# A four-layer decoder step: the scores of a pair of heads and the recurrent layer's sample part with full-array matrix products

## The chip, the cores and the metric

The kernel runs on one core of a Trainium2 chip, as one program. The metric is device time in microseconds (us), the median of several executions; lower is better. The engines are TensorE (PE in the profile, its weight loads PEld), VectorE (DVE), ScalarE (ACT), GpSimd (POOL) and SyncE (SP, which here issues nearly all DMAs). PE multiplies a stationary operand (at most 128 rows by 128 columns, loaded ahead of the product) with a moving one and adds into PSUM.

## What is computed

One inference step of a decoder with four layers of kinds A, B, C, A, for two groups that share the weights: a prompt of 256 tokens, and 8 samples of 8 new tokens each. The model is 2048 wide. Every layer is `x = x + mixer(rmsnorm(x)) @ w_out`, with an input projection that also makes a gate z.

```
A (attention):  32 heads of 64, 4 key heads; window 128; sink in the softmax
    prompt: blocks of 128 queries against the block itself and the one before
    s = q k / 8, masked;  p = softmax with sink;  o = p v
C (recurrent, 16 heads, keys 128, values 128, chunks of 32):
    b = cumsum(log f);  q_t = q exp(b);  k_intra = k exp(-b)
    o = q_t S + causal(q_t k_intra) v;   S' = exp(b_last) S + k_state v
    o = rmsnorm(o) * norm_g;   y = (silu(z) * o) @ w_out
```

Layer B is a gated convolution and is not touched. All is float32. The outputs are the last hidden states of both groups, the key and value windows, and the convolution and recurrent states.

## The kernel before

**Main stream.** Tokens lie along the free dimension: 256 of the prompt and 64 of the samples, 320 columns. `run_step` (L184 to L220) makes two output tiles of 128 features from 16 k tiles. Float32 weights and activations are split into an upper and a lower part that are exact in PE's float32r form (`w_split`, L167: ACT makes the upper part at L176, DVE or, in some steps, POOL the lower part at L177), and each product is three: upper by upper (L212), upper by lower (L213), lower by upper (L214). With 132 steps that is 12672 products of 128 x 128 weights with 320 columns. The weights stream from HBM in pieces of 128 x 1024; four raw, three upper and three lower pieces are held.

**Side work.** Everything else (rotary, scores, softmax, recurrence, gates, norms) is written as generators in eight lanes (`Lanes`), which are advanced a little at each tick of the main stream, so its small matrix products come to stand between the main ones. A pool of four PSUM slots `sm` serves them. The program is then put in order by a scheduler that simulates its time; each engine runs its own list in that order.

**Scores** (`att_unit`, L461). A unit takes one query tile `o` of a pair of key heads: 2 layers x 2 pairs x 4 groups x 2 tiles. The two heads of a pair lie on the upper and the lower 64 partitions. `qd[kv]` holds both parts of one head's queries on 128 partitions, `ql` the lower parts of both heads on their own halves; `kk` holds both parts of the keys, and `kb` only the upper parts, each head on its own half and zero elsewhere, so that one product with `ql` serves both heads. Before, `kb` is made for the first block of 128 keys (L372 to L374, L406). For the first block of queries L475 multiplies `ql` with `kb` (256 columns) and L477 adds one product a head. For the second block (256 keys a head) L480 multiplies `qd[kv]` with `kk`, and L481 adds, for each head, a product of 64 rows: the head's own half of `ql` with the same half of `kk`. L487 then adds the mask and takes the maximum on DVE.

**Recurrent layer** (`layer_c`, L792; `gla`, L930; `norm`, L1079). Each of 16 heads has three products on the samples' 64 tokens that are not full: L991 multiplies keys and queries (64 weight columns, 64 moving columns), L1017 the samples' attention with their values (64 weight columns), L1095 transposes 64 rows of the output. They are float32, which the profile shows as two records each, except for the transposes. L980 and L981 are the prompt's attention, L993 the state, L1014 to L1016 the prompt's output, L1093 and L1094 its transposes, L944 to L949 other transposes.

Of the kernel before, what the change touches and what calls it, by code (L numbers as in the profile page):

```python
# [18 lines left out]
NB = 8  # L19
# [9 lines left out]
LC_CM, LC_CMS, LC_SC, LC_BM, LC_BU, LC_ATS, LC_W, LC_AT, LC_END = 0, 128, 192, 512, 516, 524, 652, 652, 1164  # L29
# [3 lines left out]
class Pool:  # L33
    """A tag of a tile pool with a fixed number of slots, counted while tracing."""
# [29 lines left out]
class Lanes:  # L64
    """Side work traced between the matrix products of the main stream, a little at each tick."""
# [32 lines left out]
# steps in which Pool computes a share of the weights' lower parts: the vector engine has the attention to do  # L98
POOL_STEPS = set(range(2, 14)) | set(range(68, 86)) | set(range(108, 122))
# the softmax parts (head, query block) that the scalar engine normalizes  # L100
NORM_A = ((0, 0),)
# ticks between the stages of the side work
# [3 lines left out]
def trunk_kernel(ctx, tc, ins, outs):  # L106
# [77 lines left out]
    def run_step(getx, evac):  # L184
        """Two output tiles [128, NTOK]: 16 k tiles by 3 exact-part products each."""
# [7 lines left out]
        def order(k):  # L193
            # the program's last products: one tile ends before the other
            if final and k >= 12:
                return [(kk, k // 2 - 6) for kk in range(12 + 2 * (k % 2), 14 + 2 * (k % 2))] if k < 16 else []
            return [(k, 0), (k, 1)]
# [29 lines left out]
    def rsqrt(x, out, t, scratch_engine=None):  # L227
        """out = 1/sqrt(x), all [128, n] float32; x and t are overwritten."""
# [22 lines left out]
    def make_h(p, li, o):  # L251
        """Split x * ln_g of tile m into its exact parts, and add its squares up."""
# [35 lines left out]
    def split_y(p, o, y):  # L288
        """y float32 [128, NTOK] into the parts of tile (p, o)."""
        A.activation(out=yH[p][:, o, :], in_=y, func=ACTF.Copy)  # L290
        V.tensor_tensor(out=yL[p][:, o, :], in0=y, in1=yH[p][:, o, :].bitcast(F), op=ALU.subtract)
        ydone.add(2 * p + o)

    def evacuate(ps, words=NTOK):
        """The two output tiles times 1 / rms of their tokens."""
# [6 lines left out]
    def gate(w):  # L302
        """w = w (1 + tanh(w / 2)) = 2 silu(w)."""
# [52 lines left out]
    def layer_a(li):  # L356
# [7 lines left out]
        # cached keys, new keys, cached keys: the first of a pair of samples, and the second from the new keys on  # L364
# [3 lines left out]
        # keys (pair, head of the pair): exact parts over the partitions, the head's own half holds the upper one;  # L368
        # values (key block, pair, head of the pair): parts along the columns, in the same order
        kk = bg.get([128, 2, 2, TP], R)  # L370
        vp = bg.get([128, 2, 2, 2, 128], R)
        # the upper parts of the first key block, the two heads of a pair beside each other on their own halves  # L372
        kb = bg.get([128, 2, 2, 128], R)
        A.activation(out=kb, in_=ident.unsqueeze(1).to_broadcast([128, 4, 128]), func=ACTF.Copy, scale=0.0)  # L374
# [22 lines left out]
        def k_evac(ps):  # L397
            for o in range(2):
                yield from wait(wk, 2)
                a = rope(ps[o])  # L400
                for kv in range(2):
# [4 lines left out]
                    A.activation(out=kb[own, o, kv, :], in_=a[own, 0:128], func=ACTF.Copy)  # L406
# [6 lines left out]
            # the queries from here on are taken times -1/8: scores are negative, their minimum guards the softmax  # L413
# [47 lines left out]
        def att_unit(pr, gp, qd, ql):  # L461
# [5 lines left out]
            for o in range(2):  # L467
# [4 lines left out]
                # the first block of both heads and the second of the first, then the second of the second  # L472
                Sa, Sb = sm.get([128, 512]), sm.get([128, 256])
                S = [[Sa[:, 0:128], Sa[:, 256:512]], [Sa[:, 128:256], Sb]]
                T.matmul(out=Sa[:, 0:256], lhsT=ql[:, o, 0:128], rhs=kb[:, pr, :, :], start=True, stop=False)  # L475
                for kv in range(2):
                    T.matmul(out=S[kv][0], lhsT=qd[kv][:, o, 0:128], rhs=kk[:, pr, kv, 0:128], start=False, stop=(kv == 1))  # L477
                for kv in range(2):
                    sl = slice(64 * kv, 64 * kv + 64)
                    T.matmul(out=S[kv][1], lhsT=qd[kv][:, o, 128:256], rhs=kk[:, pr, kv, :], start=True, stop=False)  # L480
                    T.matmul(out=S[kv][1], lhsT=ql[sl, o, 128:256], rhs=kk[sl, pr, kv, :], start=False, stop=True)  # L481
                for kv in range(2):
# [7 lines left out]
                    sm.free()  # L490
# [63 lines left out]
        def smp_job(pr):  # L554
            while not (kdone[0] and vdone[0]):
                yield 1
            for hb in range(2):
                yield from wait(dyn, 9)
                # a pair of samples: cached keys, new keys of both, cached keys
# [6 lines left out]
                # the new values of four samples by token: upper, lower, upper parts  # L566
# [13 lines left out]
                for b2 in range(2):  # L580
# [41 lines left out]
                    # the pair's new keys are rows 16 * b2 and on: the mask clears the rest  # L622
# [169 lines left out]
    def layer_c(li):  # L792
# [4 lines left out]
        # the samples' attention, over the identity  # L797
        attss = [lc[:, LC_ATS + 64 * i:LC_ATS + 64 * i + 64] for i in range(2)]
        # the samples' queries for each half of the samples: columns (part, half, token), zero in the other half
# [36 lines left out]
        def c_pair(p):  # L836
# [18 lines left out]
            def f_evac(ps):  # L855
                yield from wait(wk, 5)
                ws = evacuate(ps)
                for o in range(2):
                    h = 2 * p + o
                    yield from wait(wk, 3)  # L860
                    q, f = st["q", o], ws[o]
# [15 lines left out]
                    st["k", o] = (ki, P)  # L877
# [9 lines left out]
        def gla_prep(h, q, ki, P, v):  # L887
# [3 lines left out]
            # products of the chunks' last decays: between chunks, to the end of a tile, from its start  # L891
# [447 lines left out]
```

## Time and profile before

| | |
|---|---|
| three runs | 2116.04, 2118.27, 2119.67 us; median 2118.27 |
| profiled execution | span 2113.5 us from the first to the last instruction; the page has no other time of it |
| busy | PE 2083.0 us (99%), weight loads 2040.2 (97%), DVE 1419.5 (67%), ACT 1007.6 (48%), POOL 684.8 (32%) |
| granted TensorE clock, mean | 0.995 of full speed |
| HBM | 153 GB/s over the span |

The page is of one execution. PE's products are pipelined, and a record's duration is not what the product costs: the next one starts well before its end. What a product costs is the time from its start to the start of the next, which the timeline shows; merged rows (x2, x4) stand for several records of one line. A product's form is given as rows * columns of its weights, then rows x columns of the moving operand (128*64 128x64: 128 rows and 64 columns of weights, 64 columns moving).

### The profile page before, as it was taken

To read this page: it belongs to the slowest core of one execution; us is meant where nothing else is said; L and a number is where in the kernel's file an instruction comes from. 1 tells how busy PE (TensorE), PEld (TensorE's weight loads), DVE (VectorE), ACT (ScalarE), POOL (GpSimd) and SP (SyncE) were. 2 spreads that over 40 slices of the span, in tenths; PEclk is the share of its full clock that TensorE was granted. 3 is DMA by queue.
4 is the path that set the end of the run, shared out by engine and by line. 5 is a ranking of instruction groups with operands and counts; after the bars stand their busy time and mean duration, and the time that the engine had idled before them with its cause. 6 is when DMAs were issued, how large, how long until landed. Compare 5 with 4: busy or idle time off the path is not lost.

```text
span 2113.5 us, 36996 instructions
## 1 busy us (share of the span) xinstructions
PE 2083.0 (99%) x14026; PEld 2040.2 (97%) x14026; DVE 1419.5 (67%) x2752; ACT 1007.6 (48%) x2034; POOL 684.8 (32%) x1002
## 2 busy tenths in 40 slices
PE   7999999999999999999999999999999999999997
PEld 7999999999999999999999999999999999999997
DVE  8778765564455545455878888888865677877644
ACT  5667654433333333344354544455444357675442
POOL 4676500110000000012545565435401156752010
PEclk9999999999999999999999999999999999999999
DMA  6433565444444444455454444454465543435542
GB/s 216 131 129 120 182 187 173 149 147 150 150 150 151 149 151 150 153 169 171 145 164 151 162 152 146 148 171 142 143 211 175 167 147 127 131 122 174 174 150 101
DMA packets 105866, 326.45 MB, mean 154 GB/s; under 512 B 16536, under 2 KB 24472, under 8 KB 105688
## 3 DMA queue, kind: packets, MB, share of 16 engines
q1 hardware_dynamic: 104968, 322.78, 48.0%
q8 instruction: 110, 1.80, 0.3%
q10 hardware_dynamic: 720, 1.31, 0.2%
q14 instruction: 68, 0.56, 0.1%
HBM read 301.88 MB, written 22.17 MB: 153 GB/s over the span
## 4 chain that ended last, share of the span: by engine, by line
PE 91%; DVE 6%; POOL 1%; issue 1%; ACT 0%; DMA 0%; SPq 0%; DVEq 0%; POOLq 0%; ACTq 0%
PE mm L214 27%; PE mm L213 27%; PE mm L212 27%; PE sm L518 1%; DVE wlp L177 1%; PE sm L481 1%; PE sm L540 1%; PE sm L480 1%; PE sm L1067 1%; DVE bg L1037 1%; DVE wk L873 0%; PE sm L981 0%; PE sm L993 0%; PE sm L595 0%; DVE hp L259 0%
## 5 line engine op out<-in xcount | busy, mean ns | idle before, releaser
L213 PE MATMUL mm<-hp,whp 128*128 128x320 f32 x3200 | 997.5, 312 | 5.8 <-DVE hp L259 5.8
L212 PE MATMUL mm<-hp,whp 128*128 128x320 f32 x3200 | 996.0, 312 | 6.3 <-ACT hp L258 6.3
L214 PE MATMUL mm<-hp,wlp 128*128 128x320 f32 x3200 | 994.1, 311 | 0.7 <-DVE wlp L177 0.7
L176 ACT ACTIVATE whp<-raw 128x1024 fp32r<-128x1024 f32 (+1 forms) x531 | 559.4, 1054 | 836.3 <-PE mm L213 675.3
L177 DVE TENSOR_TENSOR wlp<-raw,whp 128x1024 fp32r<-128x1024 f32 (+1 forms) x487 | 610.1, 1254 | 471.3 <-ACT whp L176 465.1
L213 PEld LDWEIGHTS mm<-hp,whp 128*128 128x128 f32 x3200 | 603.3, 189 | 11.1 <-DVE hp L259 7.5
L212 PEld LDWEIGHTS mm<-hp,whp 128*128 128x128 f32 x3200 | 602.4, 189 | 8.7 <-ACT hp L258 6.3
L214 PEld LDWEIGHTS mm<-hp,wlp 128*128 128x128 f32 x3200 | 602.6, 188 | 3.9 <-DVE wlp L177 1.1
L213 PE MATMUL mm<-dyn,whp 128*128 128x320 f32 x1024 | 316.5, 309 | 0.0
L212 PE MATMUL mm<-dyn,whp 128*128 128x320 f32 x1024 | 316.4, 309 | 0.0
L214 PE MATMUL mm<-dyn,wlp 128*128 128x320 f32 x1024 | 316.4, 309 | 0.0
L273 POOL TENSOR_TENSOR acc<-acc,wk 128x320 f32<-128x320 f32 x69 | 75.6, 1096 | 462.2 <-ACT wk L272 459.5
L213 PEld LDWEIGHTS mm<-dyn,whp 128*128 128x128 f32 x1024 | 192.2, 188 | 0.1
L214 PEld LDWEIGHTS mm<-dyn,wlp 128*128 128x128 f32 x1024 | 192.2, 188 | 0.0
L212 PEld LDWEIGHTS mm<-dyn,whp 128*128 128x128 f32 x1024 | 192.2, 188 | 0.0
L177 POOL TENSOR_TENSOR wlp<-raw,whp 128x1024 fp32r<-128x1024 f32 x44 | 108.5, 2466 | 102.7 <-ACT whp L176 101.7
L503 POOL TENSOR_SCALAR wk<-wk,tiny 128x256 f32<-128x256 f32 (+1 forms) x96 | 97.8, 1033 | 42.7 <-DVE tiny L496 23.4
L747 POOL COPY wk<-wk 128x2 f32<-128x2 f32 x16 | 2.9, 184 | 296.8 <-DVE wk L737 296.8
L492 ACT ACTIVATE wk<-wk,tiny 128x128 f32<-128x128 f32 (+1 forms) x128 | 57.0, 446 | 24.4 <-DVE tiny L487 24.4
L259 DVE SCALAR_TENSOR_TENSOR hp<-xo,pv,hp 128x320 fp32r<-128x320 f32 x64 | 66.2, 1072 | 2.2 <-ACT hp L258 2.2
L1064 POOL TENSOR_TENSOR dyn<-bg,dyn 128x512 fp32r<-128x512 f32 x32 | 49.0, 1556 | 49.4 <-ACT dyn L1063 49.3
L487 DVE CUSTOM_DVE_ANT_0 wk<-sm,lcp,nsink 128x128 f32<-128x128 f32 (+1 forms) x128 | 46.4, 414 | 26.0 <-PE sm L481 25.8
(250 smaller groups left out, 2163.3 us busy)
## 6 DMA issues: line engine op xcount, KB each, us to landing
raw<-in_a_w_in_dram SPq DMA_DIRECT2D x143, 512.0 KB, 3.5
raw<-in_b_w_in_dram SPq DMA_DIRECT2D x128, 512.0 KB, 3.5
raw<-in_c_w_in_dram SPq DMA_DIRECT2D x128, 512.0 KB, 3.5
raw<-in_a_w_out_dram SPq DMA_DIRECT2D x64, 512.0 KB, 3.5
raw<-in_b_w_out_dram SPq DMA_DIRECT2D x32, 512.0 KB, 3.5
raw<-in_c_w_out_dram SPq DMA_DIRECT2D x32, 512.0 KB, 3.5
bg<-in_s_dram SPq DMA_DIRECT2D x16, 512.0 KB, 4.3
out_hgrn_s_dram<-bg SPq DMA_DIRECT2D x16, 512.0 KB, 2.6
```

The source lines that it names most:

```text
L176: A.activation(out=h[:, k:k + n], in_=t[:, k:k + n], func=ACTF.Copy)
L177: e.tensor_tensor(out=l[:, k:k + n], in0=t[:, k:k + n], in1=h[:, k:k + n].bitcast(F), op=ALU.subtract)
L212: T.matmul(out=ps[o], lhsT=a, rhs=xh, start=(kk == 0), stop=False)
L213: T.matmul(out=ps[o], lhsT=a, rhs=xl, start=False, stop=False)
L214: T.matmul(out=ps[o], lhsT=b, rhs=xh, start=False, stop=(kk == 15))
L259: V.scalar_tensor_tensor(out=l, in0=x, scalar=g, in1=h.bitcast(F), op0=ALU.mult, op1=ALU.subtract)
L273: G.tensor_tensor(out=acc, in0=acc, in1=t, op=ALU.add)
L480: T.matmul(out=S[kv][1], lhsT=qd[kv][:, o, 128:256], rhs=kk[:, pr, kv, :], start=True, stop=False)
L487: V.tensor_tensor_reduce(out=p[:, c], in0=S[kv][blk], in1=maskp[:, c], scale=1.0, scalar=nsink[:, 32 * j + h:32 * j + h + 1], op0=ALU.add, ...
L492: A.activation(out=p[:, c], in_=p[:, c], func=ACTF.Exp, scale=-1.0, bias=mx[:, kv, blk:blk + 1], accum_out=sums[:, kv, blk:blk + 1])
L503: G.tensor_scalar(out=p[:, c], in0=p[:, c], scalar1=sums[:, kv, blk:blk + 1], scalar2=None, op0=ALU.mult)
L1064: G.tensor_tensor(out=sl, in0=src, in1=sh.bitcast(F), op=ALU.subtract)
```

## The change

**Scores.** `kb` is made for all 256 keys. The first block's products are as before, in a slot of their own. For the second block one product of `ql` with `kb` (128 rows, 512 columns, both heads beside each other, L478 in the new numbering) takes the place of the two products of 64 rows; the two L480 add to it. Both PSUM slots are given back after the second head's maximum, where one was given back after each head's.

**Recurrent layer.** The samples' keys get 64 zero columns behind them (one POOL memset a head, L864 in the new numbering), and their product (now L994) has 128 weight columns. The samples' attention lies in a tile of 128 columns whose right half is zero, with the identity copied to its lower left once (two POOL copies); its product with the values (now L1020) has 128 weight columns. The output tile then has 128 rows in all three blocks, so the three squares, the copy (one in place of two), the scaling and the transposes (now L1094, three alike) run over 128 rows, and the memset of the sums goes.

```diff
-LC_CM, ..., LC_AT, LC_END = 0, 128, 192, 512, 516, 524, 652, 652, 1164
+LC_CM, ..., LC_AT, LC_ATZ, LC_END = 0, 128, 192, 512, 516, 524, 652, 652, 1164, 1420
...
-        kb = bg.get([128, 2, 2, 128], R)
-        A.activation(out=kb, in_=ident.unsqueeze(1).to_broadcast([128, 4, 128]), func=ACTF.Copy, scale=0.0)
+        kb = bg.get([128, 2, 2, TP], R)
+        A.activation(out=kb, in_=ident.unsqueeze(1).to_broadcast([128, 8, 128]), func=ACTF.Copy, scale=0.0)
...
-                    A.activation(out=kb[own, o, kv, :], in_=a[own, 0:128], func=ACTF.Copy)
+                    A.activation(out=kb[own, o, kv, :], in_=a[own, 0:TP], func=ACTF.Copy)
...
-                Sa, Sb = sm.get([128, 512]), sm.get([128, 256])
-                S = [[Sa[:, 0:128], Sa[:, 256:512]], [Sa[:, 128:256], Sb]]
-                T.matmul(out=Sa[:, 0:256], lhsT=ql[:, o, 0:128], rhs=kb[:, pr, :, :], start=True, stop=False)
+                Sa, Sb = sm.get([128, 2, 128]), sm.get([128, 2, TP])
+                S = [[Sa[:, kv, :], Sb[:, kv, :]] for kv in range(2)]
+                T.matmul(out=Sa, lhsT=ql[:, o, 0:128], rhs=kb[:, pr, :, 0:128], start=True, stop=False)
                 for kv in range(2):
                     T.matmul(out=S[kv][0], lhsT=qd[kv][:, o, 0:128], rhs=kk[:, pr, kv, 0:128], start=False, stop=(kv == 1))
+                T.matmul(out=Sb, lhsT=ql[:, o, 128:256], rhs=kb[:, pr, :, :], start=True, stop=False)
                 for kv in range(2):
-                    sl = slice(64 * kv, 64 * kv + 64)
-                    T.matmul(out=S[kv][1], lhsT=qd[kv][:, o, 128:256], rhs=kk[:, pr, kv, :], start=True, stop=False)
-                    T.matmul(out=S[kv][1], lhsT=ql[sl, o, 128:256], rhs=kk[sl, pr, kv, :], start=False, stop=True)
+                    T.matmul(out=S[kv][1], lhsT=qd[kv][:, o, 128:256], rhs=kk[:, pr, kv, :], start=False, stop=(kv == 1))
...
-                    sm.free()
+                    if kv:
+                        sm.free(2)
...
-        attss = [lc[:, LC_ATS + 64 * i:LC_ATS + 64 * i + 64] for i in range(2)]
+        attss = [lc[:, LC_ATZ + 128 * i:LC_ATZ + 128 * i + 128] for i in range(2)]
+        for t in attss:
+            G.tensor_copy(out=t[64:128, 0:64], in_=lc[64:128, LC_ATS:LC_ATS + 64])
...
-                ws = evacuate(ps)
+                ws = evacuate(ps, NTOK + NB * TS)
...
-                    q, f = st["q", o], ws[o]
+                    q, kz, f = st["q", o], ws[o], ws[o][:, 0:NTOK]
+                    G.memset(kz[:, NTOK:], 0.0)
...
-            T.matmul(out=b[0:64, 256:320], lhsT=ki[:, TP:NTOK], rhs=q[:, TP:NTOK], start=True, stop=True)
+            T.matmul(out=b[:, 256:320], lhsT=ki[:, TP:NTOK + NB * TS], rhs=q[:, TP:NTOK], start=True, stop=True)
...
-            V.copy_predicated(out=ats[0:64], mask=cmask_s, data=b[0:64, 256:320])
+            V.copy_predicated(out=ats[0:64, 0:64], mask=cmask_s, data=b[0:64, 256:320])
...
-            T.matmul(out=ob[0:64, 2, :], lhsT=ats, rhs=vs, start=True, stop=True)
+            T.matmul(out=ob[:, 2, :], lhsT=ats, rhs=vs, start=True, stop=True)
...
-            V.memset(ss, 1.0)
-            for i, n in ((0, 128), (1, 128), (2, 64)):
-                A.activation(out=sq[0:n], in_=ob[0:n, i, :], func=ACTF.Square, accum_out=ss[0:n, i:i + 1])
-            A.activation(out=o[:, 0:2, :], in_=ob[:, 0:2, :], func=ACTF.Copy)
-            A.activation(out=o[0:64, 2, :], in_=ob[0:64, 2, :], func=ACTF.Copy)
+            for i in range(3):
+                A.activation(out=sq, in_=ob[:, i, :], func=ACTF.Square, accum_out=ss[:, i:i + 1])
+            A.activation(out=o, in_=ob, func=ACTF.Copy)
...
-            T.transpose(out=pt[:, 256:320], in_=o[0:64, 2, :], identity=ident[0:64, 0:64])
+            for i in range(3):
+                T.transpose(out=pt[:, i * 128:(i + 1) * 128], in_=o[:, i, :], identity=ident)
```

The scheduler puts the whole program in a new order, but at the places that count the pieces stand much as they did. PE, the first unit of scores in the first layer (`sm` is a score slot, `bg` the keys, `dyn` the queries), before:

```order
L475 MATMUL sm_799<-bg_144,dyn_733 128x256
L477 MATMUL sm_799<-bg_142,dyn_731 128x128
L477 MATMUL sm_799<-bg_142,dyn_732 128x128
L480 MATMUL sm_799<-bg_142,dyn_731 128x256
L481 MATMUL sm_799<-bg_142,dyn_733 128x256
L480 MATMUL sm_800<-bg_142,dyn_732 128x256
L481 MATMUL sm_800<-bg_142,dyn_733 128x256
```

and now:

```order
L475 MATMUL sm_799<-bg_144,dyn_733 128x256
L477 MATMUL sm_799<-bg_142,dyn_731 128x128
L477 MATMUL sm_799<-bg_142,dyn_732 128x128
L478 MATMUL sm_800<-bg_144,dyn_733 128x512
L480 MATMUL sm_800<-bg_142,dyn_731 128x256
L480 MATMUL sm_800<-bg_142,dyn_732 128x256
```

Two products of 64 rows that stood behind a full one each are replaced by one full product ahead of both. In other units more main products than before stand between these.

PE, the output of the recurrent layer's first head (`wk`, `xo`, `lcp` its operands), before:

```order
L1014 MATMUL sm_11548<-xo_11411,lcp_10791 128x128
L1015 MATMUL sm_11548<-xo_11411,lcp_10791 128x128
L1016 MATMUL sm_11548<-wk_11461,wk_11292 128x128
L1017 MATMUL sm_11548<-wk_11421,lcp_10791 64x128
L1034 MATMUL sm_11562<-xo_11431,xo_11420 128x512
```

and now:

```order
L1017 MATMUL sm_11536<-xo_11399,lcp_10775 128x128
L1018 MATMUL sm_11536<-xo_11399,lcp_10775 128x128
L1019 MATMUL sm_11536<-wk_11449,wk_11280 128x128
L1020 MATMUL sm_11536<-wk_11409,lcp_10775 128x128
L1035 MATMUL sm_11548<-xo_11419,xo_11408 128x512
```

The order is the same; the product on the samples writes 128 rows where it wrote 64.

POOL, where the recurrent layer's first pair of heads begins (`wk` the forget gates, `wlp` the lower parts of a weight piece), before:

```order
L273 TENSOR_TENSOR acc<-acc,wk_10822 128x320
L177 TENSOR_TENSOR wlp_11047<-raw_10914,whp_11046 128x1024
L866 TENSOR_TENSOR wk_11124<-wk_11120,lcp_10791 128x320
L867 TENSOR_TENSOR wk_11125<-wk_11120,wk_11124 128x320
L896 COPY tiny_11276<-wk_11126 128x8
```

and now:

```order
L273 TENSOR_TENSOR acc<-acc,wk_10808 128x320
L864 MEMSET wk_11106 128x64
L177 TENSOR_TENSOR wlp_11033<-raw_10900,whp_11032 128x1024
L864 MEMSET wk_11107 128x64
L869 TENSOR_TENSOR wk_11111<-wk_11106,lcp_10775 128x320
L870 TENSOR_TENSOR wk_11112<-wk_11106,wk_11111 128x320
```

The first new memset stands ahead of the weight split, the second behind it.

## Rows read from the trace of the kernel before

**Rows 1.** The page's busy times (share of the span) and instructions.

```profile
PE 2083.0 (99%) x14026; PEld 2040.2 (97%) x14026; DVE 1419.5 (67%) x2752; ACT 1007.6 (48%) x2034; POOL 684.8 (32%) x1002
```

**Rows 2.** Waits of PE, longest first: total us, times, longest us.

```profile
PE mm L212 <- ACT hp L258: 6.3, 1, 6.3
```

**Rows 3.** Timeline of PE, two units of scores: start us, us, what.

```profile
70.14 0.28 PE L475 MATMUL sm<-bg,dyn 128*128 128x256 f32 x1
70.25 0.34 PE L477 MATMUL sm<-bg,dyn 128*128 128x128 f32 x2
70.43 0.33 PE L480 MATMUL sm<-bg,dyn 128*128 128x256 f32 x1
70.69 0.38 PE L481 MATMUL sm<-bg,dyn 64*128 64x256 f32 x1
71.00 0.39 PE L480 MATMUL sm<-bg,dyn 128*128 128x256 f32 x1
71.31 0.38 PE L481 MATMUL sm<-bg,dyn 64*128 64x256 f32 x1
...
73.22 0.42 PE L212 MATMUL mm<-hp,whp 128*128 128x320 f32 x1
73.47 0.31 PE L213 MATMUL mm<-hp,whp 128*128 128x320 f32 x1
```

**Rows 4.** Timeline of PE, a product with 96 rows.

```profile
303.35 0.28 PE L637 MATMUL sm<-wk,wk 96*128 96x256 f32 x1
303.47 0.61 PE L639 MATMUL sm<-wk,dyn 128*128 128x128 f32 x4
```

**Rows 5.** Timeline of PE, keys by queries of the samples in the recurrent layer.

```profile
1062.55 0.33 PE L991 MATMUL sm<-wk,wk 128*64 128x64 f32 x2
1062.80 0.71 PE L993 MATMUL sm<-xo 128*128 128x128 f32 x4
1063.27 0.39 PE L214 MATMUL mm<-hp,wlp 128*128 128x320 f32 x1
1063.50 0.31 PE L212 MATMUL mm<-hp,whp 128*128 128x320 f32 x1
1063.65 0.31 PE L213 MATMUL mm<-hp,whp 128*128 128x320 f32 x1
```

**Rows 6.** Timeline of PE, 512-column products of the attention.

```profile
97.76 0.63 PE L540 MATMUL sm<-dyn,bg 128*128 128x512 f32 x2
98.23 0.39 PE L542 MATMUL sm<-dyn,bg 128*128 128x256 f32 x2
```

**Rows 7.** Timeline of PE, the recurrent layer's output.

```profile
1101.99 0.38 PE L1016 MATMUL sm<-wk,wk 128*128 128x128 f32 x2
1102.30 0.43 PE L1017 MATMUL sm<-wk,lcp 128*64 128x128 f32 x2
1102.66 0.41 PE L213 MATMUL mm<-hp,whp 128*128 128x320 f32 x1
1102.91 0.31 PE L214 MATMUL mm<-hp,wlp 128*128 128x320 f32 x1
```

**Rows 8.** Timeline of PE, the transposes of the recurrent layer's output.

```profile
1284.49 0.27 PE L1093 MATMUL sm<-ident,wk 128*128 128x128 f32 x1
1284.60 0.27 PE L1094 MATMUL sm<-ident,wk 128*128 128x128 f32 x1
1284.81 0.27 PE L1095 MATMUL sm<-ident,wk 64*128 64x64 f32 x1
1285.01 0.41 PE L214 MATMUL mm<-hp,wlp 128*128 128x320 f32 x1
```

**Rows 9.** Busy us (instructions) by engine in two stretches, then clock, DMA share, GB/s.

```profile
150.00:200.00 50.00, 50.00 (x336) 47.55 (x336) 43.20 (x122) 37.32 (x111) 35.49 (x46) 1.00 0.44 136
1100.00:1200.00 100.00, 98.43 (x657) 93.61 (x655) 86.03 (x196) 49.95 (x117) 58.80 (x109) 1.00 0.48 160
```

**Rows 10.** Waits of POOL from 1030 to 1300 us: total, times, longest.

```profile
POOL wlp L177 <- ACT whp L176: 37.8, 6, 16.3
```

More of the change, by code (lines that the diff above doesn't have):

```diff
@@ L28 @@
 LA_MASK, LA_SMASK, LA_C, LA_S, LA_PM, LA_W, LA_KV, LA_BD = 0, 384, 648, 968, 1288, 1292, 1292, 1548
-LC_CM, LC_CMS, LC_SC, LC_BM, LC_BU, LC_ATS, LC_W, LC_AT, LC_END = 0, 128, 192, 512, 516, 524, 652, 652, 1164
+LC_CM, LC_CMS, LC_SC, LC_BM, LC_BU, LC_ATS, LC_W, LC_AT, LC_ATZ, LC_END = 0, 128, 192, 512, 516, 524, 652, 652, 1164, 1420
 LW = 1932
@@ L876, in f_evac @@
                     V.scalar_tensor_tensor(out=q, in0=q, scalar=0.5, in1=P, op0=ALU.mult, op1=ALU.mult)
-                    st["k", o] = (ki, P)
+                    st["k", o] = (kz, P)
             def i_evac(ps):
@@ L1082, in norm @@
             rsqrt(ss, r, t)
-            for i, n in ((0, 128), (1, 128), (2, 64)):
-                V.tensor_scalar(out=o[0:n, i, :], in0=o[0:n, i, :], scalar1=r[0:n, i:i + 1], scalar2=None,
-                                op0=ALU.mult)
+            for i in range(3):
+                V.tensor_scalar(out=o[:, i, :], in0=o[:, i, :], scalar1=r[:, i:i + 1], scalar2=None, op0=ALU.mult)
             tiny.free(3)
@@ L1091, in norm @@
                 on[h // 2] = xo.get([128, 2, NTOK])
-            pt = sm.get([128, NTOK])
-            T.transpose(out=pt[:, 0:128], in_=o[:, 0, :], identity=ident)
-            T.transpose(out=pt[:, 128:256], in_=o[:, 1, :], identity=ident)
-            T.transpose(out=pt[:, 256:320], in_=o[0:64, 2, :], identity=ident[0:64, 0:64])
-            A.activation(out=on[h // 2][:, h % 2, :], in_=pt, func=ACTF.Copy)
+            pt = sm.get([128, 384])
+            for i in range(3):
+                T.transpose(out=pt[:, i * 128:(i + 1) * 128], in_=o[:, i, :], identity=ident)
+            A.activation(out=on[h // 2][:, h % 2, :], in_=pt[:, 0:NTOK], func=ACTF.Copy)
             sm.free()
```

## The prediction

> **What bounds the kernel now.** I read the busy totals first: PE is busy 99% of the span, DVE 67%, ACT 48%, POOL 32% [rows 1]. A busy PE need not be a limiting one, so the waits that PE itself had come next. The largest group of them is one wait of 6.3 us for the first tile [rows 2], and all of PE's idle time is 2113.5 - 2083.0 = 30.5 us, start and end of the program included. So the time is the sum of what PE's instructions cost one after the other, and each ns taken from the side products comes off the end, as long as the other engines keep up.
>
> The next question is what one product costs. The mean durations of a group are no help, because products overlap: a record lasts 0.3 to 0.4 us and the next starts after 0.15. I read start to start from the timeline instead. In the score products of one pair of heads, the reader sees this [rows 3]. The 256-column product at L475 holds PE for 0.11 us (70.14 to 70.25), the two 128-column products at L477 for 0.18 together. Then the first full product at L480 takes 0.26, the half-height one at L481 0.31, and the second L480, of the same 128 x 128 form and 256 columns as L475, 0.31. The main product behind the second unit still takes 0.25 (73.22 to 73.47), where an undisturbed one takes 0.15 (1063.50 to 1063.65) [rows 5]. So a 256-column product costs nearly three times its price wherever PE goes from a full array to 64 rows or back, on the full product as much as on the half one. A form that is merely not full does not pay: the product with 96 rows and 256 columns takes 0.12 [rows 4]. The 64-column forms of the recurrent layer do pay. Of the two records at L1016, which should take 0.22 (0.11 each, the price of a 128-column product of this kind at L1093 [rows 8]), 0.31 passes; L1017 takes 0.36; the main product behind them 0.25 [rows 7]. L1094 and L1095 take 0.21 and 0.20, where L1093 takes 0.11 [rows 8].
>
> **The change, part by part.**
>
> *Scores.* A unit is one query tile of a pair of heads: 2 layers x 2 pairs x 4 groups x 2 tiles = 32. Before: two units run from 70.14 to 73.22, and the main product behind them loses 0.10, so 3.18 us, 1.59 for one [rows 3]. After: L475 0.11, two L477 0.18, then one 512-column product and two L480, all of full form. The trace has the 512-column form at L540: two take 0.47 us, so 0.235 [rows 6]; the L480 are priced as L475 at 0.11. Sum 0.745. Saved 0.845 a unit, **27.0 us** for 32. The columns that pass are the same 1536; only the switches go. The bounds are narrow: two L477 with a main product between them may cost less than 0.18, but hardly less than the 0.11 of the same 256 columns at L475, which can add 0.07 x 32 = 2.2 us.
>
> *Recurrent layer, 16 heads.* Each of the three places is costed with its entry (extra time of the product ahead), itself, and its exit (extra time of the one behind).
> L991 (keys against queries of the samples): itself 0.25 (1062.55 to 1062.80); behind it the four L993 and the main product take 0.47 and 0.23, against 4 x 0.11 + 0.15 = 0.59, so an exit of 0.11 [rows 5]; its entry I take as L1016's 0.09. After: two records of 128 x 128 with 64 columns. No row shows such a form. From above it is 0.11 each, the 128-column price; from below 0.09, half of the two L477, which are the cheapest full-array products that I read. I take 0.11, since that row is of the same kind of operand. Saved 0.45 - 0.22 = 0.23, 3.7 us for 16.
> L1017: 0.09 + 0.36 + 0.10 [rows 7], after it 0.22. Saved 0.33, 5.3 us.
> L1095: 0.10 + 0.20, and an exit of 0.10 as behind L1017; after it 0.11 [rows 8]. Saved 0.29, 4.6 us.
> Together **13.6 us**, and 0.6 more at the lower bound of L991.
>
> *What is hidden.* On ACT the keys' second halves are copied too (four copies of 256 in place of 128 columns a layer), the zeroing doubles, and per head two copies become one; on DVE 16 small memsets go; on POOL come 16 memsets of 64 columns, two copies and a longer memset. ACT's 52% and POOL's 68% of idle time cover these [rows 1], and if that cover were gone they would cost a few us. Both score slots in PSUM are now given back together, after the second head's maximum; in the stretch of the scores PE waits for nothing, so I cost that at nothing.
>
> *What comes late next.* In 1100 to 1200 us PE was already idle for 1.57 us and DVE had 13.97 us free [rows 9]. Three heads in that stretch give 3 x 0.85 = 2.6 us, so DVE's free time falls to 11.4. If PE's waits grow as the free time shrinks, they become 1.92, and 0.35 for 3 heads is **1.9 us given back** for 16. That is an estimate. In the scores (150 to 200 us) PE has no idle time and DVE 6.8 us free for the 3.4 that four units save [rows 9]; nothing is given back there.
>
> *A rule against this change.* The rows show the half-height product at 0.31 us and the 512-column one at 0.235, so one padded product is cheaper than either of the two it replaces. The Trainium skill's page TensorEngine Tiling (Array Packing), section Overview, says that a contraction of at most 64 can be run on independent tiles, up to twice as fast, which speaks for keeping the halves. By that rule the two halves would take one 256-column time together, 0.11, and the padded product would add 0.12 x 32 = 4 us. The trace does not bear it out: a full product stands between the two halves, and their starts are 0.62 us apart [rows 3].
>
> **Sum.** 27.0 + 13.6 - 1.9 = 38.7 us. The profiled execution has a span of 2113.5, which becomes 2074.8. The median of the three runs is 2118.27, 4.8 us above that span; the profile gives no other time of that execution, so I carry the 4.8 over: **2079.6 us**.
>
> **The rivals.**
>
> *DVE becomes the bound.* It is busy 43.2 of 50 us in 150 to 200 and 86.0 of 100 in 1100 to 1200 [rows 9], and it makes the weights' lower parts that PE needs. If 0.86 is all that it can do, PE gains nothing in those stretches: the four units there and their four twins in the second attention layer, 8 x 0.845 = 6.8, and half of the heads' gain, 6.8. Time 2093. Against it: the rest of the program has slack, and lower parts can be made ahead in three buffers. Chance 0.10.
>
> *The switches stay.* If the cost did not come from the array's form but from something that the change keeps (the operand with two heads on two halves, the bank), the new L478 would cost what L480 and L481 do now. Then only one product fewer is paid for, and the time is 2110 to 2118. For it: 96 rows pay nothing, so not every odd form does. Against it: L475 has the operands of the new product, and costs 0.11 when only full products stand beside it. Chance 0.02.
>
> *Slower: POOL is held at the new memset.* It stands in POOL's queue ahead of a weight split at L177 that PE's main products need. A split waits for ACT up to 16.3 us now [rows 10], so POOL is at times long idle ahead of one. But if the memset waits for its buffer's last reader, and each of the 18 splits in this layer comes late enough to hold PE, the gain is gone from 38.7 / 18 = 2.15 us each on. At 3 us each the time is 2079.6 + 54 = 2134. Against it: splits are made up to three pieces ahead, and a piece is 24 products of 0.15, 3.5 us. Chance 0.04.
>
> *Halves that overlap.* If the two products at L481 ran beside each other in one 256-column time and no switch were paid for, the change would add (0.235 - 0.11) x 32 = 4 us: 2122. That is the rule above as a mechanism of this kernel. The rows exclude nearly all of it. Chance 0.01.
>
> **How the numbers follow.** The forecast has 0.83. Its own range: all bounds in favour (2.2 + 0.6, and 1.9 not given back) give 2074.9, and the runs shown reach 2.2 below their median, so it starts at **2073**; with a few us more of waits it ends at 2086. To hold 8 in 10 with the first rival's milder part, I end it at **2090**. A measurement of this kernel can tell about 0.2%, 4 us, from no change. Faster by more than that: forecast, first rival and the better half of the second, 0.94. Within it: the worse half of the second and half of the last, 0.02. Slower: the third rival and half of the last, 0.04.
>
> **What would show it.** Right: in the timeline after, L478 at 0.23 to start of the next, L480 at 0.12, and main products at 0.15 right behind a unit; at the three places of the recurrent layer 0.11 for each record, and no record of PE with 64 rows or 64 columns but the last few of the program. PE stays 99% busy. Wrong: L478 or the L480 behind it above 0.3; PE's idle time grown by 10 us or more; or POOL's split at L177 named as what main products wait for.

## The result, and the profile after

The changed kernel takes 2092.8 us in the median of four runs (2090.01 to 2095.0), against 2118.05 (2116.04 to 2119.67) before. The ratio is 0.9879 [0.9865, 0.9893], so 25.3 us are saved where 38.7 were forecast; the time lies 2.8 us above the range. The sign was right, and a third of the gain is missing.

The page's busy times of the changed kernel, to be read against [rows 1]; its span is 2093.1 us:

```profile
PE 2050.7 (98%) x13994; PEld 2033.0 (97%) x13994; DVE 1422.0 (68%) x2736; ACT 1006.7 (48%) x2018; POOL 678.0 (32%) x1020
```

PE's idle time has grown from 30.5 to 2093.1 - 2050.7 = 42.4 us, the 10 us or more that the prediction named as a sign of being wrong. The waits of PE say where (total, times, longest):

```profile
PE sm L1094 <- DVE wk L1085: 9.9, 5, 3.7
PE mm L213 <- DVE hp L259: 7.0, 5, 1.9
PE mm L212 <- ACT hp L258: 6.6, 1, 6.6
PE mm L212 <- DVE wk L298: 4.8, 4, 2.2
```

The same view of the kernel before:

```profile
PE mm L213 <- DVE hp L259: 5.8, 5, 1.7
PE sm L1093 <- DVE wk L1084: 4.9, 4, 1.7
```

L1094 after is L1093 before, the first transpose of the recurrent layer's output: its wait has doubled. The wait for L298, the evacuation of a pair of main output tiles, is new. L258 and L259 are the start of the program.

**The products became cheap nearly as forecast.** Timeline of PE after, two units of scores (start, us, what), for [rows 3]:

```profile
72.80 0.28 PE L475 MATMUL sm<-bg,dyn 128*128 128x256 f32 x1
72.92 0.34 PE L477 MATMUL sm<-bg,dyn 128*128 128x128 f32 x2
73.09 0.45 PE L478 MATMUL sm<-bg,dyn 128*128 128x512 f32 x1
73.38 0.40 PE L480 MATMUL sm<-bg,dyn 128*128 128x256 f32 x2
73.61 0.28 PE L475 MATMUL sm<-bg,dyn 128*128 128x256 f32 x1
...
74.43 0.31 PE L212 MATMUL mm<-hp,whp 128*128 128x320 f32 x1
74.58 0.31 PE L213 MATMUL mm<-hp,whp 128*128 128x320 f32 x1
```

A unit takes 0.81 here, and the main product behind it 0.15 again. L478 takes 0.29 right behind the two short L477, and 0.23 where something stands between. Timeline of PE after, the recurrent layer, for [rows 5] and [rows 7]:

```profile
1055.67 0.33 PE L994 MATMUL sm<-wk,wk 128*128 128x64 f32 x2
1055.84 0.66 PE L996 MATMUL sm<-xo 128*128 128x128 f32 x4
...
1094.32 0.39 PE L1020 MATMUL sm<-wk,lcp 128*128 128x128 f32 x2
1094.46 0.39 PE L213 MATMUL mm<-hp,whp 128*128 128x320 f32 x1
```

L994 takes 0.17 (0.22 forecast), L1020 0.14 and a main product behind it that gives up 0.08.

**The new wait.** Timeline of DVE (above) and of PE (below) after, in the first layer; in brackets the idle time before and what ended it:

```profile
257.21 1.23 DVE L177 TENSOR_TENSOR wlp<-raw,whp 128x1024 fp32r<-128x1024 f32 x1 [1.27 <-ACT whp L176]
260.73 1.23 DVE L177 TENSOR_TENSOR wlp<-raw,whp 128x1024 fp32r<-128x1024 f32 x1 [2.29 <-PE sm L595]
261.87 0.35 DVE L601 CUSTOM_DVE_ANT_0 wk<-sm,lcp,nsink 128x136 f32<-128x136 f32 x1
...
262.43 0.88 DVE L298 TENSOR_TENSOR wk<-mm,rb 128x320 f32<-128x320 f32 x2
```

```profile
260.10 0.63 PE L595 MATMUL sm<-dyn,lcp 128*128 128x136 f32 x4
262.97 0.41 PE L212 MATMUL mm<-hp,whp 128*128 128x320 f32 x1 [2.24 <-DVE wk L298]
```

The sample part's L595 now stands exactly at the end of a step of the main stream. The next main product needs the pair of PSUM tiles that L298 empties, and on DVE a second weight split stands ahead of L298; the split itself comes late, after 2.29 us of waiting that the profile puts down to L595. In the kernel before, the same L595 stood at main product 44 of the 96 of its step, PE had main products to do meanwhile, and DVE's order was another:

```profile
259.44 1.23 DVE L177 TENSOR_TENSOR wlp<-raw,whp 128x1024 fp32r<-128x1024 f32 x1 [1.16 <-ACT whp L176]
262.42 0.36 DVE L601 CUSTOM_DVE_ANT_0 wk<-sm,lcp,nsink 128x136 f32<-128x136 f32 x1 [1.75 <-PE sm L595]
...
262.98 0.89 DVE L298 TENSOR_TENSOR wk<-mm,rb 128x320 f32<-128x320 f32 x2
264.00 1.22 DVE L177 TENSOR_TENSOR wlp<-raw,whp 128x1024 fp32r<-128x1024 f32 x1
```

The second attention layer has the same wait at 1900.4 us. The windows ahead of it and behind it (PE, PEld, DVE, ACT, POOL busy, then granted clock) show PE at a lower clock for a while afterwards:

```profile
1890.00:1900.00 10.00, 10.00 (x73) 9.98 (x72) 5.22 (x6) 4.78 (x7) 2.88 (x2) 1.00 0.50 158
1902.60:1905.80 3.20, 3.19 (x16) 3.19 (x17) 3.03 (x12) 1.73 (x7) 0.00 (x0) 0.73 0.45 160
```

There, 12 main products start 0.27 apart in place of 0.15, so this wait costs 2.24 and 12 x 0.12 = 1.4 us more.

**The wait at the transposes.** Windows of the recurrent layer, before and after (two kernels, two fences; the first two times are the window and PE's busy time):

```profile
1000.00:1640.00 640.00, 634.34 (x4241) 614.88 (x4240) 506.45 (x1019) 307.95 (x640) 291.26 (x476) 0.99 0.49 159
```

```profile
1000.00:1640.00 640.00, 628.70 (x4283) 620.58 (x4282) 511.91 (x1008) 308.33 (x626) 286.71 (x490) 0.99 0.48 161
```

PE is idle for 5.66 us before and 11.30 after. Timeline of DVE, POOL and PE after, around the longest of these waits:

```profile
1105.50 0.17 DVE L237 SCALAR_TENSOR_TENSOR tiny<-tiny,tiny 128x3 f32<-128x3 f32 x1
...
1106.10 2.36 DVE L237 SCALAR_TENSOR_TENSOR tiny<-tiny,tiny 128x3 f32<-128x3 f32 x1
1106.10 2.33 POOL L177 TENSOR_TENSOR wlp<-raw,whp 128x1024 fp32r<-128x1024 f32 x1
...
1108.93 0.69 DVE L237 SCALAR_TENSOR_TENSOR tiny<-tiny,tiny 128x3 f32<-128x3 f32 x1
1109.65 0.85 DVE L1085 TENSOR_SCALAR wk<-wk,tiny 128x128 f32<-128x128 f32 x3
1110.12 0.92 PE L1094 MATMUL sm<-ident,wk 128*128 128x128 f32 x3 [3.73 <-DVE wk L1085]
```

The norm's chain of small operations leads to L1085 and the transposes. One L237 of three elements a partition takes 0.17 us, and the next 2.36, just as long as the weight split that POOL does beside it; with the third, of 0.69, that is 2.7 us of delay in a wait of 3.73. PE comes to these transposes 7.7 us earlier than in the kernel before (at 1106.4 against 1114.1 us), but DVE is done with L1085 only 3.8 us earlier (1110.5 against 1114.3).

### The profile page after: what moved, and what is told of

Same layout as the page of the kernel before. It is cut to its first block, busy times and chain, and to the rows that moved or that the text cites. A ratio compares the mean times of both kernels' runs of the same rounds, so it can differ in the third digit from the quotient of the medians.

```text
span 2093.1 us, 36938 instructions
## 1 busy us (share of the span) xinstructions
PE 2050.7 (98%) x13994; PEld 2033.0 (97%) x13994; DVE 1422.0 (68%) x2736; ACT 1006.7 (48%) x2018; POOL 678.0 (32%) x1020
## 4 chain that ended last, share of the span: by engine, by line
PE 89%; DVE 8%; issue 1%; POOL 1%; ACT 1%; DMA 1%; SPq 0%; DVEq 0%; POOLq 0%; ACTq 0%
PE mm L213 27%; PE mm L212 27%; PE mm L214 27%; DVE wlp L177 2%; PE sm L518 1%; PE sm L1068 1%; PE sm L540 1%; DVE tiny L237 0%; DVE wk L876 0%; DVE bg L1038 0%; PE sm L984 0%; DVE hp L259 0%; PE sm L480 0%; PE sm L478 0%; PE sm L1094 0%
## 5 line engine op out<-in xcount | busy, mean ns | idle before, releaser
L177 DVE TENSOR_TENSOR wlp<-raw,whp 128x1024 fp32r<-128x1024 f32 (+1 forms) x487 | 617.5, 1269 | 463.0 <-ACT whp L176 457.8
L259 DVE SCALAR_TENSOR_TENSOR hp<-xo,pv,hp 128x320 fp32r<-128x320 f32 x64 | 66.3, 1073 | 2.6 <-ACT hp L258 2.6
L974 POOL TENSOR_TENSOR xo<-xo,lcp 128x512 fp32r<-128x512 f32 x32 | 33.9, 1064 | 81.6 <-DVE xo L967 79.8
```

The costliest lines, as they stand in the source:

```text
L177: e.tensor_tensor(out=l[:, k:k + n], in0=t[:, k:k + n], in1=h[:, k:k + n].bitcast(F), op=ALU.subtract)
L259: V.scalar_tensor_tensor(out=l, in0=x, scalar=g, in1=h.bitcast(F), op0=ALU.mult, op1=ALU.subtract)
L974: G.tensor_tensor(out=t, in0=kv[:, u, 1, :].bitcast(F).unsqueeze(1).to_broadcast([128, 4, 128]), in1=umask[:, 4 * u:4 * u + 4].unsqueeze(2 ...
```

## The experiments

Two theories stood at first. **T1**: the products cost what was forecast, and the missing part is lost in two new waits (L298 in the attention layers, L1085 in the recurrent one) that the new order and an earlier PE make. **T2**: one part of the change saves less than its price. Each run is compared with runs of the kernel before on the same chip (2115.7 to 2118.2 us in the three batches), so runs of different batches are compared by their ratios; 0.001 is 2.1 us.

**Scores alone** (the diff's hunks of the recurrent layer undone):

```diff
-        attss = [lc[:, LC_ATZ + 128 * i:LC_ATZ + 128 * i + 128] for i in range(2)]
+        attss = [lc[:, LC_ATS + 64 * i:LC_ATS + 64 * i + 64] for i in range(2)]
...
```

> The change's scores alone; the recurrent layer as before. Theory (the switches are gone as priced, and the lost part went to new waits that the new order makes at the end of each attention layer, 2.2 us twice with a slow clock behind them, and to the start): 25 us gained in the two attention stages, some 10 given back at their ends and at the start, time 2100 to 2104, with PE waiting at L212 for DVE's evacuation at L298 near 260 and 1910 us as in the full change. Rival (nothing but run-to-run scatter and the vector engine as a bound of the recurrent layer): the scores alone give their whole 25 to 27 us, time 2091 to 2093, no such wait.

2100.33 us (2096.82 to 2103.12), ratio 0.9919 [0.9901, 0.9938]. Both waits for L298 are there (2.24 us each), and a wait of 2.25 at the transposes of a recurrent layer that the edit left as it was.

**Recurrent layer alone** (the hunks of the attention undone):

```diff
-                T.matmul(out=Sb, lhsT=ql[:, o, 128:256], rhs=kb[:, pr, :, :], start=True, stop=False)
...
+                    T.matmul(out=S[kv][1], lhsT=ql[sl, o, 128:256], rhs=kk[sl, pr, kv, :], start=False, stop=True)
```

> The change's recurrent layer alone; the scores as before. Theory (13 us of switches gone there, about half given back while PE waits for the normalization at the transposes): 2109 to 2113. Rival (the parts disturb each other only together): the whole 13 us, 2104 to 2106. The wait of PE for L1085's counterpart should be 5 us or more by the theory, as little as before by the rival.

2108.01 us (2105.08 to 2110.23), ratio 0.9957 [0.9941, 0.9973], between the two. No wait for L298; PE waits 9.2 us for L1085. The two gains, 0.0081 and 0.0043, add up to 0.0124, the whole being 0.0121: neither part spoils the other.

**The transposes' place** (the changed kernel, with the norm's transposes 24 ticks of the main stream later):

```diff
-            yield 4
+            yield 28
             yield from wait(sm)
```

> The full change, with the transposes of the recurrent layer's output written 28 ticks behind the normalization in place of 4, so that they come one stage later in PE's order; the same work. Theory (PE's order puts the transposes ahead of main products at a place where DVE is not done, so PE stands still though it has main work): PE's 9.9 us of waits there and the slow clock behind them go, time 2083 to 2087. Rival (DVE cannot do the recurrent layer's work faster, and PE would wait somewhere else): 2091 to 2095, with the waits named at another line.

2082.02 us (2081.17 to 2082.96), ratio 0.9834 [0.9819, 0.9848]. The waits for L1085 are gone, PE's idle time in 1000 to 1640 us falls to 5.2, and the waits for L298 stay.

**Halves beside each other** (the kernel before, with the two products of 64 rows behind both full ones):

```diff
                 for kv in range(2):
-                    sl = slice(64 * kv, 64 * kv + 64)
                     T.matmul(out=S[kv][1], lhsT=qd[kv][:, o, 128:256], rhs=kk[:, pr, kv, :], start=True, stop=False)
+                for kv in range(2):
+                    sl = slice(64 * kv, 64 * kv + 64)
```

> The kernel before, with the two half-height products of a unit beside each other (both full products first), so that PE changes its form twice a unit in place of four times; nothing padded. Switch theory: the second full product costs its price again and the second half product no more than 0.12, so 0.45 us a unit less, 14 us in all before anything is given back, time 2103 to 2108. If the two halves also run at the same time (starts almost equal): 3 to 4 us more, 2100 to 2104. Rival (a half-height product is slow by itself, 0.31 wherever it stands): only 0.2 a unit, 6 us, 2111 to 2113.

2112.09 us (2110.82 to 2115.3), ratio 0.9977 [0.9968, 0.9987]: a time in the rival's range, but not by the rival's mechanism. Timeline of PE in this run:

```profile
70.56 0.45 PE L479 MATMUL sm<-bg,dyn 128*128 128x256 f32 x2
70.94 0.38 PE L482 MATMUL sm<-bg,dyn 64*128 64x256 f32 x2
71.25 0.39 PE L475 MATMUL sm<-bg,dyn 128*128 128x256 f32 x1
```

The two L482 start 4 ns apart and take 0.31 together, what one of them took in [rows 3]; so in 26 of the 32 units, the others having main products in between. A unit takes 1.1 us: less than the 1.55 of the kernel before, more than the padded form's 0.8, since a change of form into the halves and one out of them stay. Start to start, the products of all 32 units fall from 47.2 to 34.1 us, close to the 14 that the switch theory asked for; the time falls by 4.6. Here too PE waits for L298 (5.0 us in four), although nothing is padded: the wait belongs to the order, with this group (L596 in this run's numbering) at the end of a step again. Behind the two long ones, 23 main products start 0.27 apart, some 3 us more, so that 5 of the 13 are left.

**The sample part's place** (one tick more between passes of the sample part; here on the run with 28 ticks, then on the changed kernel as it was):

```diff
-Y = {"spt": 7, "spv": 7, "qk": 5, "pt": 9, "pv": 6}
+Y = {"spt": 7, "spv": 8, "qk": 5, "pt": 9, "pv": 6}
```

> The run with 28 ticks ahead of the norm's transposes (2082.0 us), and one number more: the ticks between the values' passes in the sample part (Y["spv"]) go from 7 to 8. On PE the groups at L595 then no longer stand exactly at a step boundary (main products 12, 13.42, 14.48 of 96 a step in place of 13.0 and 14.0), and on DVE the evacuation L298 stands right behind the two L601 as in the kernel before, with no pair of weight splits L177 ahead of it. Theory (the two waits of 2.24 us for L298 at about 260 and 1890 us, with the main products at half clock behind them, are made by this place in the order): both waits are gone, about 6 us less, 2076 to 2078. Rival (DVE has no more to give there, so that the wait turns up at another place of the same stretch): 2081 to 2083, with waits of the same sum elsewhere between 230 and 330 us.

2074.78 us (2073.22 to 2075.61), ratio 0.9792 [0.9779, 0.9805]. All waits of PE over 2 us that are left stand at the program's start and end:

```profile
PE mm L212 <- ACT hp L258: 6.2, 1, 6.2
PE mm L213 <- DVE hp L259: 4.3, 4, 1.8
PE sm L1200 <- DVE tiny L237: 2.5, 1, 2.5
PE sm L994 <- DVE wk L1075: 1.6, 1, 1.6
```

> The changed kernel (2092.8 us) with Y["spv"] 8 in place of 7 alone, the norm's 4 ticks as they are. If the waits of the attention layers (L298) and those of the recurrent layer (L1085 ahead of L1094) are two separate losses that add up, the two waits at 260 and 1900 us go and those at L1094 stay: 2086 to 2088. If what is not lost at 260 us is lost later (fixed work on DVE or POOL, with PE only arriving earlier at the next wait), 2091 to 2093.

2084.4 us (2082.94 to 2086.14), ratio 0.9838 [0.9824, 0.9851]. The waits for L298 are gone and those for L1085 stay (10.9 us). One tick is worth 0.0041 here and 0.0042 in the run above, 8.7 and 8.9 us: a loss of its own. The two waits and the low clock explain some 6 of them. Counted from main product to main product, PE takes 280.3 us from the 385th to the 1921st in the kernel before, 272.4 in the changed one and 269.5 with the tick; from the 9985th to the 12289th, in the second attention layer, it takes 397.1, 389.2 and 384.7. With 28 ticks the two changed kernels show the same four times to 0.02 us. So the tick brings 3.0 + 4.5 = 7.4 us there, and the rest lies in the start and the recurrent layer, where runs scatter. The tick was not run on the kernel before; in these two stretches that kernel's PE is never idle, so it has no such wait to lose.

**POOL's splits** (the changed kernel, in the recurrent layer all weight splits on DVE):

```diff
-POOL_STEPS = set(range(2, 14)) | set(range(68, 86)) | set(range(108, 122))
+POOL_STEPS = set(range(2, 14)) | set(range(108, 122))
```

> The changed kernel (2092.8 us) with POOL taken out of the weight splits in the recurrent layer (POOL_STEPS without the steps 68 to 85), so that DVE makes all lower parts there and POOL no longer runs beside its small norm operations. Theory A (DVE is late at L1085 because its small operations are stretched to the length of POOL's that run beside them): L237 and L1059 fall back below 0.3 us, but DVE has 18 splits of about 2 us or less more; the waits at L1094 shrink and the time is 2086 to 2092. Theory B (DVE's own load makes it late): with more load the waits at L1094 grow by some us, and the time is 2096 to 2110.

2080.19 us (2079.93 to 2081.64), ratio 0.9820 [0.9806, 0.9833]: theory A, and more than it asked for. Groups of DVE in 1000 to 1640 us (busy, mean ns), the changed kernel and then this run:

```profile
L177 DVE TENSOR_TENSOR wlp<-raw,whp 128x1024 fp32r<-128x1024 f32 x137 | 175.7, 1285 | 70.8 <-ACT whp L176 70.8
L237 DVE SCALAR_TENSOR_TENSOR tiny<-tiny,tiny 128x3 f32<-128x3 f32 x48 | 15.0, 313 | 1.2
```

```profile
L177 DVE TENSOR_TENSOR wlp<-raw,whp 128x1024 fp32r<-128x1024 f32 x159 | 199.0, 1253 | 86.3 <-ACT whp L176 84.5 <-PE sm L996 1.7
L237 DVE SCALAR_TENSOR_TENSOR tiny<-tiny,tiny 128x3 f32<-128x3 f32 x48 | 8.3, 173 | 1.2
```

DVE does 22 splits more, 23.3 us of work, and PE still waits only 0.9 us for L1085. L237 is back at its 0.17. So it was not too much to do that made DVE late. That POOL's long operations held up its short ones is shown at the longest wait, and fits the others.

**Two products of 256 columns** (in place of the one of 512, on the run with 28 ticks):

```diff
-                T.matmul(out=Sb, lhsT=ql[:, o, 128:256], rhs=kb[:, pr, :, :], start=True, stop=False)
+                for kv in range(2):
+                    T.matmul(out=S[kv][1], lhsT=ql[:, o, 128:256], rhs=kb[:, pr, kv, :], start=(kv == 0), stop=False)
```

> The run with 28 ticks ahead of the norm's transposes (2082.0 us), with the 512-column product L478 cut into two full 128 x 128 products of 256 columns, one per head, each with the keys' zeros. If only the form of the array matters, each of the two takes 0.117 start to start like L475 and L480, the unit keeps its 0.77 us and the products themselves cost within 1 us of the one of 512 columns. The L595 groups (now L596) also stand off the step boundaries (13.44 in place of 13.0 and 14.0), so by the same theory as for the run above the two waits of 2.24 us go: 2076 to 2079. If one long product was what saved time, each of the two takes 0.2 or more and the time is 2085 or above.

2081.71 us (2080.16 to 2084.04), ratio 0.9826 [0.9813, 0.984]: neither. Start to start the two take 0.26 together, against 0.25 for the one of 512, so the form of the array is what saves, not the longer product. The waits for L298 are gone, but this order has a new one in both attention layers (5.4 us in all), behind a weight split on DVE that took 3.43 us:

```profile
170.61 0.87 PE L519 MATMUL sm<-ident,wk 128*128 128x128 f32 x3 [2.72 <-DVE wk L629]
```

**The same two edits without the change.** If T1 is right that the change makes the waits at the transposes, they should be worth little in the kernel before. It got the 28 ticks, and then, apart, POOL's splits taken out:

> The kernel before (2118.1 us) with the norm's 28 ticks ahead of its transposes, and nothing of the change. In its profile PE waits little ahead of the transposes (1.57 us in 1100 to 1200 us). Theory (the waits at the transposes appear because the change lets PE run ahead of DVE and POOL): the 28 ticks are worth at most those few us here, 2113 to 2118, against 10.8 us in the changed kernel. Rival (the later place is worth as much without the change, so that it took nothing of the change's gain): 2106 to 2109.

2106.74 us (2106.21 to 2109.41), ratio 0.9957 [0.9945, 0.997]: the rival. The ticks give 0.0043 without the change and 0.0045 with it.

> The kernel before (2118.1 us) with POOL taken out of the weight splits in the recurrent layer alone. In the changed kernel this took off 12.6 us. Theory (DVE's small operations, stretched while POOL runs, make PE wait only once PE runs ahead): little to gain, 2113 to 2119. Rival (POOL's share costs as much in the kernel before): 2104 to 2107.

2109.1 us (2106.52 to 2109.22), ratio 0.9963 [0.9951, 0.9976], between the two: 0.0037 without the change, 0.0059 with it. So T1 falls for most of what these two edits give: it was there to be had before the change. With the change they give 0.0002 and 0.0022 more, 0.4 and 4.7 us, but that is no more than the noise of such a difference (about 0.003), and the edits do not take away all that PE waits for: they leave 5.2 and 2.1 us of idle time in the changed kernel's recurrent layer, and 0.5 in the kernel before.

What the change lost there is read from PE's idle time itself. Windows of two more runs whose recurrent layer is as before (scores alone, halves beside each other), then of two whose recurrent layer is changed (recurrent layer alone, one tick more in the sample part):

```profile
1000.00:1640.00 640.00, 632.17 (x4226) 612.71 (x4225) 504.56 (x1019) 305.70 (x636) 282.25 (x471) 0.99 0.48 159
1000.00:1640.00 640.00, 634.32 (x4252) 614.82 (x4251) 506.47 (x1020) 307.66 (x639) 289.81 (x474) 1.00 0.49 160
```

```profile
1000.00:1640.00 640.00, 629.48 (x4307) 622.03 (x4307) 514.07 (x1010) 311.17 (x630) 297.63 (x494) 1.00 0.50 161
1000.00:1640.00 640.00, 627.58 (x4292) 619.88 (x4291) 511.25 (x1008) 306.75 (x621) 283.27 (x487) 1.00 0.49 161
```

With the kernels before and after, PE is idle for 5.7, 7.8 and 5.7 us with the old recurrent layer and for 11.3, 10.5 and 12.4 with the new one: 5 us more.

**Together.**

> The changed kernel without POOL's splits in the recurrent layer (2080.2 us) and with Y["spv"] 8 in place of 7 (alone it took off 8.4 us). The two act in different layers, so if the losses are separate they add up: 2080.2 - 8.4 = 2071.8, so 2070 to 2074. If the wait moves on, 2077 or above.

2073.45 us (2072.6 to 2073.68), ratio 0.9797 [0.9784, 0.981].

> As the run above, with the norm's 28 ticks too. Without POOL's splits hardly a wait at the transposes is left (0.9 us for L1085, 1.1 for L177), so the later place can give at most 2 us more: 2069 to 2073; it may also cost, since the output's work is done later: up to 2076.

2071.55 us (2070.96 to 2073.01), ratio 0.9789 [0.9776, 0.9803]. The losses are separate and add up as expected. These two and the run of 2074.78 can't be told apart by their ratios; each beats both kernels by far. So T1 holds for the attention layers and for 5 us of the recurrent layer's waits, and T2 for the 4.7 us by which the products save less than their price (24.1 and 11.8 below, for 27.0 and 13.6).

## Why the prediction was wrong

**Scores, 27.0: mis-sized, 24.1 measured.** The starts of all 32 units' products, each to the next, sum to 47.24 us before and 24.30 after, and the main products behind them, where another main one follows, lose 2.42 and 1.24: (47.24 + 2.42 - 24.30 - 1.24) = 24.1. A unit cost 1.55, not the 1.59 of the one pair read, and costs 0.80, not 0.745: in the short L477 and the L478 right behind them the prices read one by one don't add up.

**Recurrent layer, 13.6: mis-sized, about 11.8 measured.** In the two kernels with 28 ticks, where few waits disturb it, the same sums (products and the main ones behind) fall from 18.1 to 13.2 for the output, from 9.9 to 5.3 for the transposes and from 30.6 to 28.2 for the products around the keys (L980 to L993). The transposes' 4.6 is exact, the output's 5.3 came to 4.9, and L991's 3.7 to 2.4: its entry, 0.09 a head taken over from L1016, came to 0.02 to 0.04 at L981.

**The scores' "nothing is given back there": the step that failed.** I read that PE has no idle time in 150 to 200 us [rows 9] and concluded that it would have none later. But cheaper units move everything behind them in the scheduler's time, and it then put the sample part at the end of a step, with a split ahead of the evacuation. That costs 7.4 us in the two attention layers, shown by taking it away twice. Alone it would have left the time inside the range; with the terms below it didn't. A stretch without idle time told nothing of the next place where two streams meet.

**Recurrent layer, 1.9 given back: mis-sized, about 5 measured, and the reason was half right.** DVE is what PE waits for there, but not for lack of free time, from which I worked the number out: with more splits DVE was earlier.

**What bounds the kernel: an omission.** The view of waits had the row L1093 <- L1084 with 4.9 us; I read the first row of that view alone [rows 2] and took PE's side products as the whole story. Moving one number in the kernel before gives 9 us.

**The sum.** The products give 24.1 + 11.8 = 35.9; less 7.4 and 5 that is 23.5, and 25.3 was measured. The two profiles' spans differ by only 20.4, since the one after is of the slowest of its four runs and loses 2.7 us up to its 201st main product, with a lower granted clock from 20 to 40 us (0.83 against 0.91) and a wait near 24 us that takes 0.7 to 0.9 or 1.95 us in runs of either order; without them the two differ by 23.1. Where both kernels have the later transposes and neither waits for L298, the change is worth 0.9957 - 0.9792 = 0.0165, 35 us; without POOL's splits 0.9963 - 0.9797 = 0.0166, the same, each within some 4 us.

**The rivals.** The switches did not stay, POOL was not held at the new memset (16 of 0.15 us, with no idle time of POOL ahead of them), and the halves overlapped only when put beside each other. "DVE becomes the bound" names the time nearest to the result, 2093, by another mechanism: DVE's order and POOL's hold on it, not its load.

## What to carry to other kernels

Where a scheduler orders the work, a gain on the bounding engine is a gain and a new order; look in that order for places where the next step's first product needs a buffer whose emptying stands behind unrelated work, and move such a place by a tick before judging the change. Run the tuning edits on the kernel before too: half of what looked like a loss of the change was an older one. Read the view of PE's waits past its first row: the 4.9 us of its third pointed at 9 us, to be had by moving one number.

## What the runs showed of the hardware

**Short DVE operations can last as long as a long one of POOL.** L237 of three elements a partition took 2.36 us beside POOL's split of 2.33, and 0.17 otherwise. The Trainium skill's page SBUF — State Buffer, section SBUF: two separate sides, says that a VectorE operation with two SBUF inputs and a GpSimd one that reads SBUF exclude each other for the whole instruction. The trace agrees: L237 reads two tiles, and without POOL's splits its mean falls from 313 to 173 ns.

**A wait of PE can cost more than itself.** Behind the wait of 3.73 us at 1106 us the granted clock was 0.50 and then 0.70, the 1.2 GHz level for part of the time, and 1.00 again from 1118 us on (windows after):

```profile
1110.20:1112.00 1.80, 1.80 (x6) 1.44 (x7) 1.60 (x2) 0.44 (x1) 1.80 (x4) 0.50 0.56 228
1112.00:1118.00 6.00, 6.00 (x33) 5.70 (x33) 0.54 (x2) 1.58 (x3) 3.92 (x14) 0.70 0.28 90
1118.00:1124.00 6.00, 6.00 (x43) 5.93 (x42) 5.14 (x11) 4.35 (x12) 2.36 (x2) 1.00 0.26 87
```

Of two equal waits of 2.24 us in the changed kernel the one at 1900 was followed by it and the one at 260 was not; in the run of the scores alone the one at 260 was, too (0.71 from 262 to 266 us).

**Two products on half the rows ran at the same time when they stood beside each other**: they started 3 to 4 ns apart and took 0.31 us together, in 26 units of the run with the halves beside each other. The prediction had given that a chance of 0.01 in the kernel's own order, rightly. Where padding is not possible it is an alternative: it took 13 us off these products.
